# An encoder block in split fp32: two more plain up-projection pairs, and operand sums of 24 activation blocks made early and kept in DRAM

## The chip, the core and the metric

The kernel runs as one program on one core of a Trainium2 chip. The metric is device time in microseconds, the median of several executions. TensorE (PE) multiplies; VectorE (DVE), ScalarE (ACT) and GpSimd (POOL) prepare and finish; SyncE (SP) issues most loads, POOL issues the saves and the accumulating loads.

## The reference

One layer of a bidirectional encoder over 512 positions of width 2048. The part that matters here is its feed-forward half:

```
x = x + concat(RMSNorm_A(attn), RMSNorm_B(conv)) @ W_o
h = RMSNorm(x)                            # 512 x 2048
u = conv3_centred(h @ W_up) + b           # 512 x 11264: 5632 gates, 5632 values
y = silu(u[:, :5632]) * u[:, 5632:]       # 512 x 5632
x = x + y @ W_down                        # 512 x 2048
out = RMSNorm(x)                          # the last one
```

All of it is float32.

## The kernel before, in words

Everything is kept transposed, 128 channels on the partitions and the 512 positions along the row. A float32 product is made of three matmuls: each operand is split into a rounded part (`hi`, a copy on ACT) and the rest (`lo`, a subtraction on DVE), and `hi·hi + hi·lo + lo·hi` is accumulated. Each weight unit of 128x1024 (512 KB) is loaded by SP into one of eight `raw` buffers and split into one of three `hi`/`lo` pairs of buffers. The program is a list of `Item`s, one for each stretch of PE work on one weight unit. `run` walks the list and keeps loads and splits a few items ahead; an item's `posts` are other work, written into the program behind the item or some items later. A scheduler of the framework then sets the final order on each engine from this; within an engine the instructions run in that order.

The feed-forward half has 44 pairs `f` of 128 gate and 128 value columns. The first `NPLAIN` pairs are plain: four items of 24 matmuls of 512 columns each (line 242). The others go through `seven`, a scheme that makes a 2x2 block product with seven products in place of eight: seven items of 24 matmuls of 256 columns each (line 864), for which weights are added and subtracted (`raw<-raw` on DVE, accumulating `raw<-wall` loads on POOL, line 888) and the operand too is needed in sums and differences of its blocks. `make_operands` builds these: from two 128x512 tiles `a` and `b` it makes differences of 256 columns (lines 229, 836, 837) and splits them into seven tiles of fp32r. One call of it is called an operand set here.

Operand sets are made in two places. Before the first `seven` pair, `normed_operands` is called eight times from posts of the plain items: it loads two tiles of the residual back from DRAM (`t<-xr`), scales them (line 828), and makes the set; all eight sets are used by every `seven` pair. In the down-projection the 44 activation blocks are taken in chunks of eight: five chunks with four output groups `m` of seven items each (`down_seven`, again line 864), and the last four blocks plain. Each of the five chunks needs four operand sets. For that, `gated` saves each finished activation block to DRAM (`act<-t`, line 780, on POOL), and `sums_of` loads two of them back (`t<-act`, line 785, on SP) and calls `make_operands`: for the first chunk from posts of the last up-projection pair, for each later chunk from posts of the chunk ahead of it, one set in each `m`. `fetch_xr` loads the residual, to which the down-projection adds, in 32 pieces (line 989) at the end of the up-projection. All 128x512 tiles (2 KB a partition) share one pool of 80 buffers.

The two places where one part hands over to the next are called the first crossing here (plain to `seven` pairs) and the second crossing (up- to down-projection).

Of the kernel before, what the change touches and what calls it, by code (L numbers as in the profile page):

```python
# [62 lines left out]
SCALE = float(1.0 / np.sqrt(np.float32(NOPE + ROPE)))  # L63
UW = 1024
NT = 80
NPLAIN = 4
AHEAD = 4
HT = T // 2
FILL = 3
# [100 lines left out]
def encoder_block(ctx: ExitStack, tc: tile.TileContext, gx, wall, vecs, rot, out):  # L170
# [9 lines left out]
    def tile_r():  # L180
        return tp.tile([P, T], F32R, tag="t", name="t")

    def pair():
        return tile_r(), tile_r()

    def ztile():
        return tp.tile([P, T], F32, tag="t", name="t")
# [36 lines left out]
    def col(name, i):  # L224
        c = _VEC[name] + i
        return vec[:, c:c + 1]

    def tt(o, a, b, op, eng=None):
        (eng or nc.vector).tensor_tensor(out=o, in0=a, in1=b, op=op)  # L229

    def split(dst, src, eng=None):
        nc.scalar.copy(out=dst[0], in_=src)  # L232
        tt(dst[1], src, dst[0].bitcast(F32), ALU.subtract, eng)
# [87 lines left out]
    items = []  # L321
# [221 lines left out]
    v, qr, qk, pr = {}, {}, {}, {}  # L543
# [227 lines left out]
    def half(t, i):  # L771
        return t[:, i * HT:(i + 1) * HT]
# [3 lines left out]
    def save(name, src):  # L776

        saved[name] = [(dram.tile([P, T], F32, name=f"{name[0]}{name[1]}_{i}"), t.dtype) for i, t in enumerate(src)]
        for (o, _), t in zip(saved[name], src):
            nc.gpsimd.dma_start(o, t.bitcast(F32))  # L780

    def restore(name):
        ts = [tp.tile([P, T], dt, tag="t", name="t") for _, dt in saved[name]]
        for o, (d, _) in zip(ts, saved[name]):
            nc.sync.dma_start(o.bitcast(F32), d)  # L785
        return ts

    def conv_up(u, t, s, f):
# [4 lines left out]
        if s == 0:  # L793
            nc.scalar.activation(u, u, AF.Silu)

    def gated(us, f):
        tt(us[1], us[0], us[1], ALU.mult)
        if f < starts[last]:
            save(("act", f), [us[1]])
            return  # L800
        a = pair()
        split(a, us[1])
        save(("act", f), a)


    def up_plain(f, by_half):

        us, its = [None, None], []
        for s in range(2):
            def conv(ps, s=s):  # L810
                t = ztile()
                us[s] = ztile()
                if s == 0:
                    tt(t, ps, rx.r, ALU.mult)
                else:
                    nc.vector.scalar_tensor_tensor(out=t, in0=ps, scalar=-1.0, in1=rx.r, op0=ALU.mult, op1=ALU.mult)
                conv_up(us[s], t, s, f)

            lag = 5 if (f, s) == (0, 0) else 1
            its.append(proj16([("up", s, f, j) for j in range(2)], h2, [(lag, conv)] + [(lag + 1, lambda ps: gated(us, f))] * s, True))  # L820
        return its

    operands = []

    def normed_operands(i):
        (a,), (b,) = restore(("xr", 2 * i)), restore(("xr", 2 * i + 1))
        for k, t in ((2 * i, a), (2 * i + 1, b)):
            nc.vector.scalar_tensor_tensor(out=t, in0=t, scalar=col("ffn_g", k), in1=rx.r, op0=ALU.mult, op1=ALU.mult)  # L828
        operands.append(make_operands(a, b))

    def make_operands(a, b):

        u, v = ztile(), ztile()
        tt(half(u, 0), half(a, 0), half(a, 1), ALU.subtract)
        tt(half(u, 1), half(b, 1), half(a, 1), ALU.subtract)
        nc.vector.scalar_tensor_tensor(out=half(v, 0), in0=half(a, 0), scalar=-1.0, in1=half(u, 1), op0=ALU.mult, op1=ALU.subtract)  # L836
        nc.vector.scalar_tensor_tensor(out=half(v, 1), in0=half(v, 0), scalar=-1.0, in1=half(b, 0), op0=ALU.mult, op1=ALU.subtract)  # L837
        one = tile_r()
        split((half(one, 0), half(one, 1)), half(a, 0))
        got = {1: (half(one, 0), half(one, 1))}  # L840
        for src, names in ((u, (5, 7)), (v, (6, 4)), (b, (2, 3))):
            p = pair()
            split(p, src)
            for j, q in enumerate(names):
                got[q] = half(p[0], j), half(p[1], j)
        return got

    banks = []
# [87 lines left out]
    def up_seven(f):  # L936
        tg, tv, us = [], [], [None, None]

        def c11(ps):
            tg.append(ztile())  # L940
            nc.scalar.copy(out=half(tg[0], 0), in_=ps)

        def c22(ps, other):
            tv.append(ztile())
            tt(half(tv[0], 1), ps, other, ALU.add)

        def c21(ps, other):
            tt(half(tv[0], 0), ps, other, ALU.add)
            us[1] = ztile()
            conv_up(us[1], tv[0], 1, f)  # L950

        def c12(ps):
            nc.scalar.copy(out=half(tg[0], 1), in_=ps)
            us[0] = ztile()
            conv_up(us[0], tg[0], 0, f)

        units = {f"a{s + 1}{j + 1}": ("up", s, f, j) for s in range(2) for j in range(2)}
        its = seven(f, units, {"c11": c11, "c22": c22, "c21": c21, "c12": c12}, operands)
        its[-1].posts.append((2, lambda: gated(us, f)))
        return its  # L960

    starts = [sum(CHUNKS[:i]) for i in range(len(CHUNKS))]
    last = len(CHUNKS) - 1
    plain = []
    for f in range(0, NPLAIN - 2):
        plain += [it for its in up_plain(f, False) for it in its]
    four = [it for f in range(NPLAIN - 2, NPLAIN) for it in up_plain(f, True)]
    plain += [its[j] for j in range(2) for its in four]
    plain.insert(2, Item(rx.sums, posts=[(1, rx.chain)]))
    plain.insert(4, Item(rx.spread, posts=[(1, rx.take)]))  # L970
    for i in range(KD // 2):
        plain[(6, 7, 8, 9, 10, 14, 15, 16)[i]].posts.append((0, lambda i=i: normed_operands(i)))
    plain[-2].posts.append((0, mark))
    items.extend(plain)
    for f in range(NPLAIN, NF):
        items.extend(up_seven(f))


    acts, xt, sums = {}, {}, {}
# [4 lines left out]
    def fetch_xr(m):  # L984
        for a in range(2):
            for h in range(2):
                xt[m, a, h] = ztile()
                for e in range(2):
                    nc.sync.dma_start(half(xt[m, a, h], e), half(saved[("xr", 4 * m + 2 * e + a)][0][0], h))

    def sums_of(c, i):
        (a,), (b,) = (restore(("act", starts[c] + 2 * i + j)) for j in range(2))
        sums.setdefault(c, []).append(make_operands(a, b))

    def down_seven(c, m):
        def onto(a, h, op):
            def f(ps):
                tt(xt[m, a, h], xt[m, a, h], ps, op)
            return f

        units = {f"a{i + 1}{j + 1}": ("ds", c, m, i, j) for i in range(2) for j in range(2)}
        posts = {"s7": onto(1, 1, ALU.subtract), "u2": onto(1, 0, ALU.subtract), "c11": onto(0, 0, ALU.add),
                 "c22": onto(1, 1, ALU.subtract), "c21": onto(1, 0, ALU.subtract), "c12": onto(0, 1, ALU.add)}
        return seven(m, units, posts, sums.setdefault(c, []), T, True)

    at = len(items) - 7
    for i, j in enumerate((0, 2, 4, 5)):
        items[at + j].posts.append((0, lambda i=i: sums_of(0, i)))
    for m in range(KD // 4):
        items[at + (5, 6, 6, 6)[m]].posts.append((0, lambda m=m: fetch_xr(m)))  # L1010
    for c in range(last):
        for m in range(KD // 4):
            its = down_seven(c, m)
            if c + 1 < last:
                its[2].posts.append((0, lambda c=c, m=m: sums_of(c + 1, m)))
            items.extend(its)

    def fetch(f):
# [99 lines left out]
```

## Time and profile before

| | before |
|---|---|
| median of 3 runs | 2070.59 us (2070.19 to 2071.48) |
| profiled execution | 2071.46 us, its span 2069.7 us |
| mean granted TensorE clock | 0.991 |
| PE busy | 2023.5 us, 98% |
| DVE busy | 1557.1 us, 75% |
| ACT busy | 985.5 us, 48% |
| POOL busy | 212.6 us, 10% |
| HBM traffic | 140 GB/s over the span |

Shares of busy time are means over the whole program; a matmul that is slow or waits for its data can be counted as busy, so the count of matmuls in a stretch of 100 us says more on PE than its share.

### The profile page before, as it was taken

How to read it: one execution, taken by the hardware profiler on the slowest of the kernel's cores; microseconds unless marked ns; L12 is line 12 of the kernel's file. 1: busy time of each engine (PE TensorE's matmuls, PEld its weight loads, DVE VectorE, ACT ScalarE, POOL GpSimd, SP SyncE). 2: the span in 40 equal slices, each digit the busy share in tenths (PEclk: the TensorE clock that was granted, in tenths of full speed). 3: DMA queues.
4: the chain of work that ended last, by engine and by line, in shares of the span. 5: the costliest groups of instructions: out<-in, count | busy, mean ns of one | idle time of the engine just before them, and what ended most of it. 6: DMA issues, size and time to landing. Idle time of an engine off the chain costs nothing.

```text
span 2069.7 us, 34189 instructions
## 1 busy us (share of the span) xinstructions
PE 2023.5 (98%) x13970; PEld 1881.3 (91%) x13970; DVE 1557.1 (75%) x1905; ACT 985.5 (48%) x1374; POOL 212.6 (10%) x206
## 2 busy tenths in 40 slices
PE   8999999999999998999999999999998999999997
PEld 7888888888888887999999999999997999999997
DVE  7375776764557588878788787787887998988776
ACT  5253543432224345555555555555554554544454
POOL 5001323220001000000000000000000100000000
PEclk9999999999999998999999999999999999999999
DMA  7222222123444343554544545445456876767642
GB/s 260 95 87 76 79 70 89 65 92 97 140 141 139 130 160 96 153 154 132 163 134 147 160 132 158 141 140 169 130 157 193 235 197 172 207 161 212 173 123 82
DMA packets 94444, 291.85 MB, mean 141 GB/s; under 512 B 10704, under 2 KB 19024, under 8 KB 94288
## 3 DMA queue, kind: packets, MB, share of 16 engines
q1 hardware_dynamic: 77648, 230.95, 32.6%
q0 software_dynamic: 16640, 58.73, 14.6%
q8 instruction: 109, 1.79, 0.3%
q14 instruction: 47, 0.39, 0.1%
HBM read 268.66 MB, written 20.97 MB: 140 GB/s over the span
## 4 chain that ended last, share of the span: by engine, by line
PE 88%; DVE 6%; DMA 2%; issue 1%; ACT 0%; SPq 0%; DVEq 0%; ACTq 0%
PE ps L864 51%; PE ps L242 37%; DVE t L229 2%; DVE lo L229 2%; DMA t<-act 2%; DVE raw L229 1%; DMA t<-xr 0%; ACT hi L232 0%; DVE t L836 0%; DVE t L837 0%; DMA raw<-wall 0%; DVE t L828 0%; DVE t L486 0%; DVE t L487 0%; SPq L785 0%
## 5 line engine op out<-in xcount | busy, mean ns | idle before, releaser
L864 PE MATMUL ps<-t,hi 128*128 128x256 f32 x6720 | 1188.9, 281 | 26.2 <-DVE t L229 9.3
L864 PEld LDWEIGHTS ps<-t,hi 128*128 128x128 f32 x6720 | 1024.3, 189 | 30.8 <-DVE t L229 11.5
L864 PE MATMUL ps<-t,lo 128*128 128x256 f32 x3360 | 923.5, 280 | 1.7 <-DVE lo L229 1.7
L232 ACT CAST hi<-raw 128x1024 fp32r<-128x1024 f32 (+1 forms) x550 | 573.9, 1046 | 731.7 <-PE ps L864 264.1
L229 DVE TENSOR_TENSOR lo<-raw,hi 128x1024 fp32r<-128x1024 f32 (+1 forms) x549 | 676.1, 1233 | 214.4 <-ACT hi L232 204.3
L864 PEld LDWEIGHTS ps<-t,lo 128*128 128x128 f32 x3360 | 626.3, 189 | 2.4 <-DVE lo L229 2.3
L242 PE MATMUL ps<-t,hi 128*128 128x512 f32 x1968 | 613.8, 394 | 5.3 <-ACT t L237 4.5
L242 PEld LDWEIGHTS ps<-t,hi 128*128 128x128 f32 x1968 | 369.8, 188 | 87.6 <-ACT t L237 5.4
L242 PE MATMUL ps<-t,lo 128*128 128x512 f32 x992 | 385.9, 392 | 0.0
L229 DVE TENSOR_TENSOR t<-ps,t 128x512 f32<-128x512 f32 (+2 forms) x257 | 143.3, 571 | 161.7 <-PE ps L242 99.0
L229 DVE TENSOR_TENSOR t<-t 128x512 fp32r<-128x512 f32 (+4 forms) x356 | 222.6, 642 | 35.1 <-DMA t<-act 14.4
L242 PEld LDWEIGHTS ps<-t,lo 128*128 128x128 f32 x992 | 186.6, 188 | 41.9 <-issue 0.5
L229 DVE TENSOR_TENSOR raw<-raw 128x1024 f32<-128x1024 f32 x160 | 194.9, 1218 | 0.5
L242 PE MATMUL ps<-t 128*128 128x256 f32 (+1 forms) x642 | 108.7, 326 | 0.0
L232 ACT CAST t<-t 128x512 fp32r<-128x512 f32 (+2 forms) x149 | 81.9, 577 | 54.5 <-DVE t L229 28.5
L242 PEld LDWEIGHTS ps<-t 128*128 128x128 f32 x642 | 95.2, 190 | 10.3
L229 DVE TENSOR_TENSOR t<-t,ps 128x512 f32<-128x512 f32 x128 | 86.5, 681 | 18.1 <-PE ps L864 17.1
L780 POOL DMA_DIRECT2D act<-t x48 | 27.4, 571 | 698.9 <-DVE t L229 661.4
L229 POOL TENSOR_TENSOR t<-t 128x512 f32<-128x512 f32 x39 | 65.3, 1674 | 73.4 <-DVE t L229 40.1
L888 POOL DMA_DIRECT2D raw<-wall x60 | 52.2, 870 | 194.8 <-ACT t L920 71.3
L341 ACT ACTIVATE t<-l 128x512 f32<-128x512 f32 x44 | 27.5, 627 | 47.2 <-DVE l L229 47.0
L894 POOL DMA_DIRECT2D raw<-wall x20 | 17.3, 864 | 316.7 <-DVE lo L229 201.8
(81 smaller groups left out, 826.2 us busy)
## 6 DMA issues: line engine op xcount, KB each, us to landing
raw<-wall SPq DMA_DIRECT2D x372, 512.0 KB, 4.0
raw<-wall POOLq DMA_DIRECT2D x80, 512.0 KB, 5.9
act<-t POOLq DMA_DIRECT2D x48, 256.0 KB, 2.5
t<-act SPq DMA_DIRECT2D x48, 256.0 KB, 5.2
t<-gx SPq DMA_DIRECT2D x16, 256.0 KB, 3.8
xr<-l POOLq DMA_DIRECT2D x16, 256.0 KB, 2.4
t<-xr SPq DMA_DIRECT2D x16, 256.0 KB, 3.8
t<-xr SPq DMA_DIRECT2D x32, 128.0 KB, 3.8
```

Source lines behind the costliest of these rows:

```text
L229: (eng or nc.vector).tensor_tensor(out=o, in0=a, in1=b, op=op)
L232: nc.scalar.copy(out=dst[0], in_=src)
L242: nc.tensor.matmul(ps, lhsT=w, rhs=x, start=start, stop=stop)
L341: nc.scalar.activation(sq, src, AF.Square)
L780: nc.gpsimd.dma_start(o, t.bitcast(F32))
L864: nc.tensor.matmul(half(ps, e), lhsT=w[a][:, c:c + P], rhs=ops[k][q][b], start=start and e == k == i == 0, stop=k == n - 1 and i == 2, ski ...
L888: nc.gpsimd.dma_start(raw["a21"], wall[UIDX[units["a22"]]], accum_op=ALU.add)
L894: nc.gpsimd.dma_start(raw["s"], wall[UIDX[units["a12"]]], accum_op=ALU.add)
```

## The change

Two more pairs are plain (`NPLAIN` 6), and the eight calls of `normed_operands` are spread over the 26 items that the plain part now has. For the blocks of chunks 2, 3 and 4 (`f` from 16 to 39, named in `EARLY`), `gated` no longer saves the activation block: at each odd `f` it makes the operand set of the two blocks at once, in the up-projection, and saves its seven tiles (`sums`). `sums_of` then loads the seven finished tiles for these chunks; for chunks 0 and 1 it does what it did. The chunks are taken in the order 2, 0, 3, 1, 4. There are 28 operand sets in all as before; 12 of them move from the down-projection into the up-projection, so that 84 tiles of sums are saved in place of 24 blocks, and loaded in place of 24. `make_operands` now gives back its seven tiles, and `views` names their halves.

```diff
-NPLAIN = 4
+NPLAIN = 6
+ORDER = [2, 0, 3, 1, 4]
+EARLY = (2, 3, 4)
...
+    kept = {}
+
     def gated(us, f):
         tt(us[1], us[0], us[1], ALU.mult)
+        if f // 8 in EARLY:
+            kept[f] = us[1]
+            if f % 2:
+                save(("sums", f // 2), make_operands(kept.pop(f - 1), kept.pop(f)))
+            return
         if f < starts[last]:
             save(("act", f), [us[1]])
             return
...
-        operands.append(make_operands(a, b))
+        operands.append(views(make_operands(a, b)))
...
         split((half(one, 0), half(one, 1)), half(a, 0))
-        got = {1: (half(one, 0), half(one, 1))}
-        for src, names in ((u, (5, 7)), (v, (6, 4)), (b, (2, 3))):
+        ts = [one]
+        for src in (u, v, b):
             p = pair()
             split(p, src)
+            ts += p
+        return ts
...
-        plain[(6, 7, 8, 9, 10, 14, 15, 16)[i]].posts.append((0, lambda i=i: normed_operands(i)))
+        plain[(6, 7, 9, 11, 13, 18, 20, 22)[i]].posts.append((0, lambda i=i: normed_operands(i)))
...
     def sums_of(c, i):
-        (a,), (b,) = (restore(("act", starts[c] + 2 * i + j)) for j in range(2))
-        sums.setdefault(c, []).append(make_operands(a, b))
+        f = starts[c] + 2 * i
+        if c in EARLY:
+            ts = restore(("sums", f // 2))
+        else:
+            (a,), (b,) = (restore(("act", f + j)) for j in range(2))
+            ts = make_operands(a, b)
+        sums.setdefault(c, []).append(views(ts))
...
-        items[at + j].posts.append((0, lambda i=i: sums_of(0, i)))
+        items[at + j].posts.append((0, lambda i=i: sums_of(ORDER[0], i)))
...
-    for c in range(last):
+    for c, after in zip(ORDER, ORDER[1:] + [None]):
         for m in range(KD // 4):
             its = down_seven(c, m)
-            if c + 1 < last:
-                its[2].posts.append((0, lambda c=c, m=m: sums_of(c + 1, m)))
+            if after is not None:
+                its[2].posts.append((0, lambda c=after, m=m: sums_of(c, m)))
             items.extend(its)
```

The scheduler's order of the built program shows what this does at three places. The first is DVE at the first crossing. Here `t_5999` and `t_6001` are the residual tiles of the eighth (last) operand set, the rows up to `t_6023` build it, `lo_6105` is the first split of weights for a `seven` item, and L816, L486 and L487 belong to the convolution of the last plain pairs. Before:

```order
L828 SCALAR_TENSOR_TENSOR t_5999<-t_5999,vec_83,t_5394 128x512
L229 TENSOR_TENSOR t_5970<-t_5901,t_5970 128x512
L828 SCALAR_TENSOR_TENSOR t_6001<-t_6001,vec_83,t_5394 128x512
L229 TENSOR_TENSOR t_6005<-t_5999 128x256
L229 TENSOR_TENSOR t_6005<-t_6001,t_5999 128x256
L836 SCALAR_TENSOR_TENSOR t_6006<-t_5999,t_6005 128x256
L229 TENSOR_TENSOR t_6011<-t_5999,t_6011 128x256
L837 SCALAR_TENSOR_TENSOR t_6006<-t_6006,t_6001 128x256
L229 TENSOR_TENSOR t_6015<-t_6005,t_6014 128x512
L229 TENSOR_TENSOR t_6019<-t_6006,t_6018 128x512
L229 TENSOR_TENSOR lo_6105<-raw_5898,hi_6104 128x1024
L229 TENSOR_TENSOR t_6023<-t_6001,t_6022 128x512
```

After the change `t_6197` and `t_6199` are the residual tiles of the eighth set and `lo_6225` and `lo_6262` are splits of weights for the last plain items:

```order
L837 SCALAR_TENSOR_TENSOR t_6197<-t_6197,vec_83,t_5394 128x512
L231 TENSOR_TENSOR lo_6225<-raw_6078,hi_6224 128x1024
L837 SCALAR_TENSOR_TENSOR t_6199<-t_6199,vec_83,t_5394 128x512
L231 TENSOR_TENSOR t_6203<-t_6197 128x256
L231 TENSOR_TENSOR t_6203<-t_6199,t_6197 128x256
L845 SCALAR_TENSOR_TENSOR t_6204<-t_6197,t_6203 128x256
L231 TENSOR_TENSOR t_6209<-t_6197,t_6209 128x256
L846 SCALAR_TENSOR_TENSOR t_6204<-t_6204,t_6199 128x256
L231 TENSOR_TENSOR t_6213<-t_6203,t_6212 128x512
L231 TENSOR_TENSOR lo_6262<-raw_6136,hi_6261 128x1024
L231 TENSOR_TENSOR t_6217<-t_6204,t_6216 128x512
L231 TENSOR_TENSOR t_6221<-t_6199,t_6220 128x512
```

Before, the eighth set stands around the split of the first `seven` weights. After, it stands around the last splits for plain items; the four convolutions of the last plain pairs come behind it.

The second place is DVE in the up-projection at an odd `f` of `EARLY`. `t_9122` and `t_8890` are the two activation blocks, `lo_` are splits of weights; L231, L845 and L846 are lines 229, 836 and 837 of before. After:

```order
L231 TENSOR_TENSOR lo_9257<-raw_8960,hi_9256 128x1024
L231 TENSOR_TENSOR raw_9351<-raw_9190,raw_9192 128x1024
L231 TENSOR_TENSOR t_9195<-t_9122,t_8890 128x256
L231 TENSOR_TENSOR lo_9289<-raw_8993,hi_9288 128x1024
L845 SCALAR_TENSOR_TENSOR t_9196<-t_8890,t_9195 128x256
L231 TENSOR_TENSOR lo_9322<-raw_9084,hi_9321 128x1024
L231 TENSOR_TENSOR t_9201<-t_8890,t_9201 128x256
L846 SCALAR_TENSOR_TENSOR t_9196<-t_9196,t_9122 128x256
L231 TENSOR_TENSOR t_9205<-t_9195,t_9204 128x512
L231 TENSOR_TENSOR t_9209<-t_9196,t_9208 128x512
L231 TENSOR_TENSOR t_9213<-t_9122,t_9212 128x512
L231 TENSOR_TENSOR t_9358<-ps_6302,t_9262 128x256
```

The pieces of one operand set (`t_9195` to `t_9213`) stand between the splits of weights; before, the same stretch held only the splits and the sums of the weights.

On POOL, saves and accumulating loads of weights alternated, one of each for each pair; after the change, in the pairs of `EARLY`, two loads of weights in a row (line 904 of the changed kernel) are followed by the seven saves of one set (line 782).

The third place is SP at the second crossing, where L259 are loads of weights. Before:

```order
L259 DMA raw_15314<-wall 128x1024
L259 DMA raw_15371<-wall 128x1024
L785 DMA t_15242<-act0_0_5498 128x512
L785 DMA t_15244<-act1_0_5744 128x512
L259 DMA raw_15635<-wall 128x1024
L259 DMA raw_15637<-wall 128x1024
L785 DMA t_15342<-act2_0_6035 128x512
L785 DMA t_15344<-act3_0_6113 128x512
L259 DMA raw_15678<-wall 128x1024
L785 DMA t_15430<-act4_0_6347 128x512
L785 DMA t_15432<-act5_0_6581 128x512
L259 DMA raw_15734<-wall 128x1024
```

After, from the same place on (L261 are the weights; L787 is the load of `sums`):

```order
L787 DMA t_15593<-sums10_5_10219 128x512
L787 DMA t_15594<-sums10_6_10220 128x512
L261 DMA raw_15771<-wall 128x1024
L261 DMA raw_15773<-wall 128x1024
L261 DMA raw_15814<-wall 128x1024
L787 DMA t_15635<-sums11_0_10713 128x512
L787 DMA t_15636<-sums11_1_10714 128x512
L787 DMA t_15637<-sums11_2_10715 128x512
L787 DMA t_15638<-sums11_3_10716 128x512
L787 DMA t_15639<-sums11_4_10717 128x512
L787 DMA t_15640<-sums11_5_10718 128x512
L787 DMA t_15641<-sums11_6_10719 128x512
```

Before, the eight loads of `act` alternate with weights. After, the seven tiles each of `sums8`, `sums9` and `sums10` stand in one piece behind the first four weights of the down-projection, then come three weights, the seven tiles of `sums11`, and directly behind them the 32 residual loads.

## Rows read from the trace of the kernel before

**Rows 1.** Windows by stage: bounds; us, PE, PEld, DVE, ACT, POOL busy (x count); PEclk; DMA; GB/s.

```profile
600.00:700.00 100.00, 100.00 (x439) 82.12 (x438) 64.39 (x84) 38.99 (x50) 8.99 (x16) 1.00 0.42 137
700.00:800.00 100.00, 90.89 (x413) 74.50 (x412) 77.68 (x126) 42.72 (x62) 2.56 (x4) 0.95 0.38 124
800.00:900.00 100.00, 100.00 (x835) 100.00 (x834) 82.00 (x92) 55.77 (x78) 7.21 (x10) 0.98 0.50 145
900.00:1000.00 100.00, 100.00 (x852) 100.00 (x851) 80.13 (x87) 55.61 (x76) 7.15 (x10) 1.00 0.50 146
1500.00:1600.00 100.00, 90.26 (x730) 89.15 (x729) 78.46 (x97) 54.67 (x80) 7.39 (x11) 0.95 0.57 171
1600.00:1700.00 100.00, 94.70 (x795) 93.40 (x794) 95.28 (x136) 52.66 (x71) 9.79 (x12) 1.00 0.78 217
1700.00:1800.00 100.00, 98.06 (x829) 97.29 (x828) 91.52 (x127) 51.01 (x66) 7.74 (x9) 1.00 0.69 184
1800.00:1900.00 100.00, 98.25 (x831) 97.80 (x829) 84.17 (x103) 45.04 (x52) 9.43 (x11) 1.00 0.72 197
1900.00:2000.00 100.00, 100.00 (x851) 100.00 (x850) 79.44 (x88) 46.40 (x55) 7.24 (x9) 1.00 0.64 173
```

**Rows 2.** Windows again, of the matmuls of line 242, then of line 864.

```profile
700.00:800.00 100.00, 81.59 (x359) 66.47 (x357) 0.95 0.38 124
...
700.00:800.00 100.00, 9.47 (x54) 8.03 (x55) 0.95 0.38 124
```

**Rows 3.** The chain of waits at the first crossing: start, length, what.

```profile
792.95 0.66 DVE t L828
...
796.34 0.34 DVE t L837
...
798.60 1.44 PE ps L864 x5
```

**Rows 4.** The chain of waits at the second crossing.

```profile
1581.14 7.73 DMA t<-act
...
1592.10 4.63 PE ps L864 x21
1596.73 2.78 DMA t<-xr
```

**Rows 5.** Windows around the two crossings.

```profile
784.00:800.00 16.00, 6.89 (x33) 5.27 (x32) 14.03 (x25) 6.89 (x11) 0.54 (x1) 0.70 0.05 17
1570.00:1610.00 40.00, 29.50 (x209) 27.98 (x208) 31.93 (x51) 20.91 (x34) 2.86 (x4) 0.87 0.63 194
```

**Rows 6.** DVE's waits between 1560 and 1900 us: total, times, longest.

```profile
DVE t L229 <- DMA t<-act: 14.4, 15, 4.8
```

**Rows 7.** DVE's groups by form, 700 to 800 us: count, busy, mean ns.

```profile
L229 DVE TENSOR_TENSOR t<-t 128x512 fp32r<-128x512 f32 x24 | 15.9, 685 | 1.5 <-ACT t L232 1.4
...
L229 DVE TENSOR_TENSOR t<-t 128x256 f32<-128x256 f32 x16 | 6.1, 417 | 0.0
...
L836 DVE SCALAR_TENSOR_TENSOR t<-t 128x256 f32<-128x256 f32 x8 | 3.4, 422 | 0.2
```

**Rows 8.** POOL's groups by form, 900 to 1500 us.

```profile
L888 POOL DMA_DIRECT2D raw<-wall x31 | 27.1, 875 | 63.4 <-ACT t L920 61.3 <-ACT hi L232 2.0
L780 POOL DMA_DIRECT2D act<-t x31 | 17.3, 559 | 505.6 <-DVE t L229 505.6
```

**Rows 9.** SP's timeline at the second crossing: start, us spent on issuing, what.

```profile
1564.64 0.85 SPq L785 DMA_DIRECT2D t<-act  x2
...
1580.66 0.96 SPq L785 DMA_DIRECT2D t<-act  x2
...
1593.76 1.93 SPq L785 DMA_DIRECT2D t<-act  x2
1595.73 19.61 SPq L989 DMA_DIRECT2D t<-xr  x32
```

**Rows 10.** The page's DMA issues: count, KB each, us to landing.

```profile
t<-act SPq DMA_DIRECT2D x48, 256.0 KB, 5.2
```

More of the change, by code (lines that the diff above doesn't have):

```diff
@@ L839, in make_operands, with views @@
         split((half(one, 0), half(one, 1)), half(a, 0))
-        got = {1: (half(one, 0), half(one, 1))}
-        for src, names in ((u, (5, 7)), (v, (6, 4)), (b, (2, 3))):
+        ts = [one]
+        for src in (u, v, b):
             p = pair()
             split(p, src)
+            ts += p
+        return ts
+    def views(ts):
+        got = {1: (half(ts[0], 0), half(ts[0], 1))}
+        for i, names in enumerate(((5, 7), (6, 4), (2, 3))):
             for j, q in enumerate(names):
-                got[q] = half(p[0], j), half(p[1], j)
+                got[q] = half(ts[1 + 2 * i], j), half(ts[2 + 2 * i], j)
         return got
```

## The prediction

> **What bounds the kernel now.** I read the windows by stage first and counted matmuls, since their busy time is modelled and their count is not. Undisturbed, PE starts 852 matmuls of 256 columns in 100 us, one in .1174 us (the row from 900), and 439 of 512 columns, one in .2278 us (the row from 600) [rows 1]. So a `seven` pair (168 matmuls) costs 19.72 us and a plain pair (96) 21.87 us. In such stretches no other engine decides: DVE is busy 64% and 80%.
>
> The time lost lies where the counts fall short. **First crossing:** between 700 and 800 us PE did 359 wide and 54 narrow matmuls [rows 2], worth 81.8 + 6.3 us, so 11.9 us are gone; from 800 to 900 another 17 of 852 are missing, 2.0 us: 13.9 in all. **Second crossing:** between 1570 and 1610 there are 209 matmuls [rows 5] where 40 / .1174 = 341 fit: 132 missing, 15.5 us. **Chunks:** from 1500 to 1900 the rows have 730, 795, 829 and 831, so 223 missing, 26.2 us; without the crossing's 15.5 that leaves 10.7 us, spread over the first four chunks. From 1900, in the chunk that makes no operand sets, nothing is missing [rows 1]. These counts include what the lower clock after a stall costs: the granted clock was .70 of 2.4 GHz while PE starved at the first crossing and .87 around the second [rows 5].
>
> What PE waits for is read from the chains. At the first crossing it is DVE: scaling the residual (L828), differences (L837) of the last operand set and then a split of weights stand right before PE's next matmul at 798.60 [rows 3], and DVE was busy 14.0 of 16 us [rows 5]. At the second it is a DMA: DVE stands behind `t<-act` for 7.73 us, weights' splits stand behind that on DVE, and PE resumes at 1592.10 [rows 4]. Of DVE's waits from 1560 to 1900 us, 14.4 us in 15 times are for `t<-act` [rows 6].
>
> **The change, part by part.**
>
> *Two more plain pairs.* Each costs 21.87 − 19.72 = 2.15 us more PE work: **+4.3**. No cover, since PE is the bound there.
>
> *First crossing.* An operand set is three splits of 512 columns at .685 us and five operations of 256 columns at .417 to .422 [rows 7]: 3 × .685 + 5 × .418 = 4.15 us of DVE, with two scalings 5.6. The eight sets are the same, but are spread over 26 items. In the order before, the last set stands around the first `seven` split, so that all of it is on PE's path; after, it stands around `lo_6225` and `lo_6262`, the last two splits of plain weights. At least two plain items of 24 × .2278 = 5.5 us are then still ahead of PE, 11 us, against some 6 us for the rest of the set and 7 to 8 us for the four convolution passes and the first split behind it. Much fits, and little is left over. Bounds: 0 (as before) and 13.9 (all). I take 13.4: **−13.4**. If the cover were gone, the stall would come back at up to its old size.
>
> *Up-projection.* Twelve sets of 4.15 us, 49.8 us of DVE, move under two `seven` pairs each. DVE idles 19.87 in 100 us there [rows 1], so 7.8 us in two pairs (39.4 us); after the set 3.7 us are left and DVE is at 90.5%. ACT, at 56%, has room. The inputs are already in SBUF, so no load is waited for. The pieces stand between splits of weights in the order, so a split is pushed back by a few operations of .4 to .7 us, not by the whole set. The nearest row for the danger is the down-projection's own: 16 sets cost 10.7 us, .67 each; by that, 12 would cost 8.0. But DVE stood at 95% there and waited for loads [rows 1, 6], which the new place does not. Between 0 and 8.0 I take **+1.5**.
>
> *Saves.* 84 tiles on POOL in place of 24. A save takes POOL .56 us and an accumulating load .88 [rows 8]; seven saves are 3.9 us in 39.4, and in POOL's order they stand behind both loads of weights, about a pair's length before the next load. 0. The Trainium skill ("SBUF — State Buffer", section "A bandwidth-pool intuition that's wrong") speaks against this part: a DMA issued from GpSimd needs the port that DVE can hold, and its 620 ns became about 3100 ns beside a DVE copy. By it seven saves would last an estimated 21.7 us. The trace does not agree so far: the saves took .56 us beside a DVE that was 80% busy.
>
> *Second crossing.* DVE makes no set there any more, so nothing of its queue stands behind a load: the 7.73 us and what follows from them go. What can be late instead is a tile that PE itself needs. The loads of `sums8` take the place of the first `t<-act`, which SP issued at 1564.64 [rows 9], some 3 us before the last pair starts on PE (PE resumes at 1592.10 with the sixth of its products; five took 5 × 2.82 us and some 10 us of the stall, so it began at about 1568). Call that start T. 21 tiles at .48 us an issue (two in .96 [rows 9]) are 10.1 us, until T + 7. Then three loads of weights wait for their buffers, which splits free at one a product, 2.82 us; I put `sums11` at T + 14.5. Its seven issues take 3.4 us, and a tile lands 5.2 us after its issue [rows 10]: T + 23.1. PE needs it one microsecond into the first product of the down-projection, at T + 19.7 + 1.05 = T + 20.8. Late by 2.3. The 32 residual loads come behind at .61 us each [rows 9]; the first eight land at about T + 28, when the fourth product's result (T + 31) asks for them. I take 2 us of stall in place of 15.5: **−13.5**. Bounds: 0 and, with every tile issued as slowly as the slowest two (.97 each, 1.93 for two [rows 9]), 28 × .49 = 13.7 us more, so a crossing as bad as before.
>
> *Chunks.* Eight sets stay in the down-projection (for chunks 0 and 1, made while chunks 2 and 3 run) of the 16 that lay in the chunks. At .67 each: **−5.4**. Bounds: −10.7, and 0 if what remains is as crowded.
>
> Sum: 4.3 − 13.4 + 1.5 − 13.5 − 5.4 = −26.5. The profiled execution took 2071.46 us, 1.8 more than its span and .9 more than the median; so 2071.46 − 26.5 = 2045.0, or **2044** beside the median.
>
> **The rivals.**
>
> *Loads bunch at the second crossing.* 28 tiles (7.3 MB), seven weights and 32 pieces leave SP one after the other. For it: the DMA share was already .63 with 8 tiles there [rows 5], and one pair of issues took 1.93 us. Against it: three of four sets are issued 15 us ahead. At the upper bound the crossing costs 11 to 14 us more than I took: 2044 + 11 = 2055. Chance .17.
>
> *The first crossing's stall moves rather than goes.* The four convolution passes and the last set are the same DVE work, and the eighth set can only start when a tile or its residual is free; if it starts two items late, half to all of 13.9 remains: 2044 + 7 to 13, 2051 to 2057. Chance .10.
>
> *DVE becomes the bound of the up-projection* (the other side). A split for PE stands behind pieces of the set, twelve times. It is not faster any more from (26.5 − 4.1) / 12 = 1.9 us more a set than I took, and if all 4.15 lay bare, 12 × 4.15 − 1.5 = 48 us come on top: 2092. For it: the row at 95% DVE lost 6.7 us in 100 [rows 1]. Against it: 7.8 us of idle time for 4.15 of work. Chance .09, two thirds of it with a loss.
>
> *POOL is held up.* If each save took five times its .56 us, seven would take some 20 us; they start when the set is ready, some 8 us behind the last load of weights, and the next load would come 8 to 10 us late, twelve times: about 100 us slower, 2145. That is the page's rule; the saves' .56 us speaks against it. Chance .02.
>
> **How the numbers follow.** The forecast has .62, with its own range 2038 to 2051 (the up-projection's 0 to 8, the chunks' bounds). If every stall went, it would be 4.3 − 13.9 − 15.5 − 10.7 = −35.8, 2035. The first two rivals reach to 2057, both in part to 2060. Range 2035 to 2060, with some .12 above it. A measurement of this kernel tells about .2%, 4.1 us, from no change. Faster: .62 + .17 + .10 + .02 of the third = .91; same .03; slower .06.
>
> **What would show it.** First crossing: no window with under 80% of its matmuls before the `seven` pairs. Up-projection: 852 in each 100 us with DVE at 90%; under 835 the third rival is right. Second crossing: no DVE wait for a load; PE waiting for a DMA of `sums` for 0 to 3 us. Chunks: losses only in the second and third place, half of before. I am wrong if a PE wait for splits shows in each pair of `EARLY`, or if SP's issues stretch past the start of the down-projection.

## The result, and the profile after

The changed kernel took 2135.86 us (median, 2134.8 to 2136.25) against 2070.39 us of the kernel before: 65.5 us slower. The two medians make 1.0316; the ratio estimated from all runs is 1.0344 (95% interval 1.0268 to 1.042). The prediction was 2044 us, range 2035 to 2060.

The windows by stage of the changed kernel, in the columns of [rows 1], show where.

```profile
700.00:800.00 100.00, 100.00 (x441) 81.86 (x440) 75.32 (x119) 42.31 (x60) 3.11 (x5) 1.00 0.41 138
800.00:900.00 100.00, 100.00 (x770) 95.34 (x769) 79.88 (x95) 52.21 (x72) 6.34 (x9) 1.00 0.48 139
900.00:1000.00 100.00, 100.00 (x885) 100.00 (x884) 83.06 (x91) 58.35 (x81) 7.19 (x10) 1.00 0.53 156
1000.00:1100.00 100.00, 95.56 (x812) 95.16 (x811) 78.76 (x89) 54.39 (x76) 9.38 (x14) 0.97 0.52 154
1100.00:1200.00 100.00, 91.11 (x734) 90.31 (x733) 76.83 (x94) 52.40 (x75) 11.28 (x18) 0.95 0.48 144
1200.00:1300.00 100.00, 90.32 (x716) 89.30 (x714) 75.24 (x91) 49.91 (x71) 12.11 (x19) 0.93 0.49 148
1300.00:1400.00 100.00, 87.51 (x700) 86.71 (x701) 73.58 (x90) 50.41 (x76) 15.17 (x25) 0.93 0.56 164
1400.00:1500.00 100.00, 91.13 (x732) 90.12 (x731) 74.74 (x91) 51.49 (x73) 11.27 (x18) 0.95 0.51 160
1500.00:1600.00 100.00, 91.12 (x727) 90.31 (x726) 76.02 (x93) 51.76 (x74) 11.29 (x18) 0.93 0.48 143
1600.00:1700.00 100.00, 91.72 (x746) 90.73 (x745) 72.27 (x83) 47.58 (x64) 10.71 (x15) 0.97 0.88 274
1700.00:1800.00 100.00, 90.30 (x745) 89.30 (x744) 79.88 (x102) 42.96 (x54) 7.71 (x9) 0.97 0.79 235
1800.00:1900.00 100.00, 99.68 (x845) 99.44 (x844) 82.96 (x100) 45.06 (x52) 8.61 (x10) 1.00 0.73 198
```

Three things are to be seen. First, the stall of the first crossing is gone: 441 wide matmuls from 700 to 800 us, and the 770 from 800 to 900 are what the last wide ones, until about 826 us, and the narrow ones behind them make without a gap. Second, from 900 to 1000 there are 885 narrow matmuls, where the kernel before had 852 in its undisturbed stretches [rows 1]: a faster pace, at the same granted clock of 1.00. Third, from 1000 to 1600, in the pairs of `EARLY`, the counts sum to 4421 where 852 each would be 5112: 691 missing, 81 us by the .1174 us of [rows 1]. From 1600 to 1900, around and behind the second crossing, 2336 are there of 2556: 220 missing, 26 us, no less than the 26.2 us of before.

As a sum: two plain pairs +4.3, first crossing −13.9, the 33 extra matmuls of 900 to 1000 −3.9, up-projection +81.1, second crossing and chunks 25.8 − 26.2 = −.4: +67 us, for 65.5 measured (the extra matmuls before 900 us are not in it).

What PE waited for in the up-projection, from PE's waits between 1000 and 1600 us (total, times, longest):

```profile
PE ps L880 <- ACT t L936: 53.2, 12, 4.4
```

One wait, the same twelve times. L936 is the copy in `keep`, by which ACT empties a PSUM bank (a bank in which PE's products are summed; the copies are `s7` and `u2`) before PE may go on in it. ACT's timeline in one of the twelve, pair 24 (start, length, what, idle before and its releaser):

```profile
1202.47 1.05 ACT L234 CAST hi<-raw 128x1024 fp32r<-128x1024 f32 x1 [2.06 <-PE ps L880]
1205.06 1.04 ACT L234 CAST hi<-raw 128x1024 fp32r<-128x1024 f32 x1 [1.54 <-DVE lo L231]
1206.01 0.92 ACT L234 CAST t<-t 128x256 fp32r<-128x256 f32 x2
1208.07 1.14 ACT L234 CAST t<-t 128x512 fp32r<-128x512 f32 x2 [1.14 <-DVE t L846]
1209.11 0.64 ACT L936 COPY t<-ps 128x256 f32<-128x256 f32 x2
```

PE's wait of 4.4 us ended with the first of the two copies at about 1209.5, so PE had been done with all ahead of it, the products to be copied among them, since 1205.1; ACT began the copies (x2) only at 1209.11. Ahead of them on ACT stand a split of weights, which waited 1.54 us for DVE, and the operand set's four copies, the last two of which waited 1.14 us for L846 on DVE. Of the 4.0 us from 1205.1 to 1209.11 the split took 1.0, the set's copies 2.0 and the wait for DVE 1.1. PE stood still for 4.4 us, and ran at a lower clock behind it: a short window of the same place,

```profile
1208.00:1216.00 8.00, 6.47 (x35) 6.47 (x36) 1.93 (x4) 1.96 (x5) 3.29 (x6) 0.58 1.00 337
```

with 35 matmuls in 8 us (68 fit) at a mean granted clock of .58 of 2.4 GHz, that is mostly at 1.2 GHz. So each of the twelve costs 81.1 / 12 = 6.8 us, counted by 852.

At the second crossing the waits are others than before [rows 4]. PE's waits there, in three stretches (1640 to 1660, 1685 to 1700, 1755 to 1785 us):

```profile
PE ps L880 <- DMA t<-sums: 2.4, 1, 2.4
```

```profile
PE ps L880 <- ACT ps L931: 3.2, 1, 3.2
```

```profile
PE ps L880 <- ACT hi L234: 8.2, 2, 8.0
```

The first, 2.4 us for the last tiles of `sums`, is the one that the prediction priced at 2.3. The last, 8.2 us, stands in the second chunk (chunk 0). SP's timeline (start, time on issuing, what), SP's waits from 1749 to 1763 us and ACT's from 1640 to 1800 us explain it:

```profile
1629.19 14.46 SPq L787 DMA_DIRECT2D t<-sums  x21
...
1646.55 8.58 SPq L787 DMA_DIRECT2D t<-sums  x7
...
1744.13 4.39 SPq L787 DMA_DIRECT2D t<-sums  x4
1748.87 0.33 SPq L261 DMA_DIRECT2D raw<-wall  x1
1749.55 12.50 SPq L787 DMA_DIRECT2D t<-sums  x10
1762.40 1.03 SPq L787 DMA_DIRECT2D t<-act  x2
```

```profile
SPq L787 <- DMA t<-sums: 4.9, 9, 1.9
SPq L787 <- DMA raw<-wall: 4.4, 2, 3.4
```

```profile
ACT t L234 <- DMA t<-act: 15.4, 3, 12.8
```

The activation blocks of chunk 1's first operand set were issued at 1762.40, behind the tiles of chunk 3's sums. SP took 12.5 us for the last ten of these: between 1749 and 1763 us it waited 9.3 us in all for earlier loads to land. ACT stood behind these blocks for up to 12.8 us, with the weights' splits for PE behind it.

The saves on POOL cost what was said: the page's rows

```profile
L782 POOL DMA_DIRECT2D sums<-t x84 | 46.4, 552 | 38.9 <-ACT t L234 25.3
```

give .55 us each, beside the .56 of [rows 8].

### The profile page after: what moved, and what is told of

Same layout as the page of the kernel before. It is cut to its first block, busy times and chain, and to the rows that moved or that the text cites. A ratio compares the mean times of both kernels' runs of the same rounds, so it can differ in the third digit from the quotient of the medians.

```text
span 2134.5 us, 34139 instructions
## 1 busy us (share of the span) xinstructions
PE 2045.0 (96%) x13826; PEld 1892.0 (89%) x13826; DVE 1544.5 (72%) x1893; ACT 976.7 (46%) x1358; POOL 242.9 (11%) x264
## 5 line engine op out<-in xcount | busy, mean ns | idle before, releaser
L880 PE MATMUL ps<-t,hi 128*128 128x256 f32 x6496 | 1164.2, 284 | 71.5 <-ACT t L936 53.2
L234 ACT CAST hi<-raw 128x1024 fp32r<-128x1024 f32 (+1 forms) x544 | 566.6, 1046 | 809.5 <-PE ps L880 254.8
L880 PE MATMUL ps<-t,lo 128*128 128x256 f32 x3248 | 900.6, 282 | 0.0
L231 DVE TENSOR_TENSOR lo<-raw,hi 128x1024 fp32r<-128x1024 f32 (+1 forms) x543 | 668.3, 1234 | 197.6 <-ACT hi L234 187.9
L244 PE MATMUL ps<-t,hi 128*128 128x512 f32 x2096 | 653.9, 394 | 4.9 <-ACT t L239 4.7
L244 PE MATMUL ps<-t,lo 128*128 128x512 f32 x1056 | 411.0, 392 | 0.0
L231 DVE TENSOR_TENSOR t<-ps,t 128x512 f32<-128x512 f32 (+3 forms) x255 | 143.1, 575 | 233.2 <-PE ps L880 117.0
L231 DVE TENSOR_TENSOR t<-t 128x512 f32<-128x512 f32 (+4 forms) x356 | 221.5, 640 | 31.0 <-ACT t L343 10.7
L231 DVE TENSOR_TENSOR raw<-raw 128x1024 f32<-128x1024 f32 x154 | 187.9, 1220 | 0.8
L231 DVE TENSOR_TENSOR t<-t,ps 128x512 f32<-128x512 f32 x128 | 87.0, 684 | 40.8 <-PE ps L880 36.1
L231 POOL TENSOR_TENSOR t<-t 128x512 f32<-128x512 f32 x39 | 63.8, 1636 | 76.1 <-DVE t L231 40.1
L782 POOL DMA_DIRECT2D act<-t x24 | 14.3, 595 | 341.0 <-DVE t L231 283.2
L782 POOL DMA_DIRECT2D sums<-t x84 | 46.4, 552 | 38.9 <-ACT t L234 25.3
```

The costliest lines, as they stand in the source:

```text
L244: nc.tensor.matmul(ps, lhsT=w, rhs=x, start=start, stop=stop)
L880: nc.tensor.matmul(half(ps, e), lhsT=w[a][:, c:c + P], rhs=ops[k][q][b], start=start and e == k == i == 0, stop=k == n - 1 and i == 2, ski ...
```

## The experiments

Theory A: ACT's order. The set's copies stand ahead of the copies that PE waits for. Theory B: DVE has too much to do. Theory C: the saves, on POOL or as traffic. Later come theory P, that the pace follows from whether PE was interrupted, and rival Q, that it follows from the number of plain pairs or from where the tiles lie. The kernel before took 2069 to 2072 us beside each of these runs.

**Six plain pairs alone.**

```diff
-ORDER = [2, 0, 3, 1, 4]
-EARLY = (2, 3, 4)
+ORDER = [0, 1, 2, 3, 4]
+EARLY = ()
```

> Six plain pairs and the new places of the eight normed operand sets, but all 44 activation blocks saved as before, chunks in natural order, 20 sets made in the down-projection. This isolates the first crossing. All theories of the loss in the up-projection expect 852 matmuls in each 100 us there. If the first crossing's 13.9 us are gone for 4.3 us of plain work, the time is 2070.4 + 4.3 - 13.9 = 2061 (2058 to 2064); if the stall only moved, 2068 to 2075.

2034.53 us (2033.8 to 2036.45), ratio .9825 (.981 to .9839): 27 us better than expected. Its windows:

```profile
1000.00:1100.00 100.00, 100.00 (x885) 100.00 (x884) 83.44 (x91) 58.00 (x80) 7.19 (x11) 1.00 0.50 146
...
1500.00:1600.00 100.00, 88.08 (x732) 86.49 (x732) 84.80 (x113) 53.93 (x78) 10.56 (x15) 0.95 0.72 212
```

The 885 of above hold through the whole up-projection, from 826 to 1540 us; then the second crossing stalls, and the counts fall much as they did before. At 852 the same matmuls would take 714 us × (885 / 852 − 1) = 27.7 us more, about the 26.5 us that were missing from my sum.

**The operand sets written later.**

```diff
-            if f % 2:
-                save(("sums", f // 2), make_operands(kept.pop(f - 1), kept.pop(f)))
...
         its[-1].posts.append((2, lambda: gated(us, f)))
+        if f // 8 in EARLY and f % 2:
+            its[-1].posts.append((6, lambda: save(("sums", f // 2), make_operands(kept.pop(f - 1), kept.pop(f)))))
```

> The changed kernel, with the operand sets of the up-projection written four items later (posts six items behind the pair's last item in place of two), so that on ACT both copies that empty a PSUM bank for PE (the keep copies) stand ahead of the set's splits. Same work, same saves. Theory A (ACT's queue order): the twelve waits of 4.4 us of PE for the keep copy go, with the clock lost behind them, 691 missing matmuls or 81 us in all: 2055 (2045 to 2065). Theory B (DVE has too much to do there): the wait moves to a split of weights and most stays: 2100 to 2136. Theory C (the saves on POOL or their DMA traffic hold something up): 2125 to 2136.

2040.36 us (2039.6 to 2041.25), ratio .9851 (.9834 to .9867). ACT's order at pair 18, in the changed kernel and in this one (`COPY t<-ps` of L936 and L934 are the `keep` copies, `CAST t` the set's):

```
L234 CAST hi_9321<-raw_9084 128x1024
L234 CAST t_9201<-t_8890 128x256
...
L234 CAST t_9212<-t_9122 128x512
L936 COPY t_9262<-ps_9231 128x256
L936 COPY t_9294<-ps_6302 128x256
```

```
L934 COPY t_9227<-ps_9196 128x256
L234 CAST hi_9253<-raw_8993 128x1024
L934 COPY t_9259<-ps_6302 128x256
L234 CAST hi_9286<-raw_9084 128x1024
L955 COPY t_9290<-ps_9161 128x256
L234 CAST t_9329<-t_8890 128x256
```

The windows of this kernel:

```profile
1100.00:1200.00 100.00, 100.00 (x885) 100.00 (x884) 92.16 (x113) 62.57 (x90) 16.87 (x27) 1.00 0.61 193
...
1500.00:1800.00 300.00, 279.02 (x2294) 276.53 (x2293) 233.41 (x283) 133.17 (x166) 26.11 (x33) 0.97 0.78 234
...
1660.00:1680.00 20.00, 11.57 (x79) 11.07 (x78) 10.00 (x15) 4.91 (x7) 0.00 (x0) 0.75 0.84 281
```

From 1000 to 1500 us PE waits for nothing, and does 885 in each 100 us with DVE 92% busy. So B is wrong: the same work, written four items later, costs nothing there, and A holds. The set stands later on DVE too, so this run by itself does not part ACT's order from DVE's; the timeline of the twelve waits does, in which 1.1 of 4.0 us are for DVE and the rest is ACT's own work ahead of the copies. The waits also broke the faster pace, so the 81 us counted by 852 are too few: the two runs are 2135.9 − 2040.4 = 95.5 us apart. The time is below A's range because A's sum went by 852, and without the waits the pace stays at 885. It is 6 us slower than the run before nevertheless: from 1500 to 1800 there are 2294 matmuls of 2556, 31 us lost, with a wait of 8.4 us behind `t<-act` as in the changed kernel (the row from 1660).

**One keep copy ahead.** As the run before, with 4 in place of 6.

> As the run before, but the sets are written only two items later, so that on ACT the first keep copy stands ahead of the set's splits and the second behind them. Theory A: a smaller wait for the second copy, 1 to 3 us in each of twelve pairs with its clock, 2065 to 2110, between the other two. Theory B and C: no different from the changed kernel, 2125 to 2136.

2095.9 us (one run), between the two. PE's waits from 1000 to 1600 us:

```profile
PE ps L878 <- ACT hi L234: 20.2, 12, 1.8
PE ps L878 <- ACT t L934: 5.3, 13, 1.8
```

The wait shrank to at most 1.8 us, in the range given, but most of it was for a split of weights (its copy on ACT) and not for the `keep` copy: both stand behind copies of the set on ACT. Theories B and C expected no difference from the changed kernel.

**Saves without sets.** This kernel saves the two activation blocks in place of the sums, and leaves the making of the twelve sets out.

```diff
-                save(("sums", f // 2), make_operands(kept.pop(f - 1), kept.pop(f)))
+                x, y = kept.pop(f - 1), kept.pop(f)
+                save(("sums", f // 2), [x, y, x, y, x, y, x])
+                saved[("sums", f // 2)] = [(d, F32R) for d, _ in saved[("sums", f // 2)]]
```

> The changed kernel without the making of the twelve sets in the up-projection: the two activation blocks themselves are saved seven times in all in place of the seven tiles, and the down-projection multiplies these. The values are not the reference's. 84 saves on POOL and all the traffic stay, DVE's and ACT's work of the sets is gone. Theory A and B: no waits in the up-projection, 2055 (2045 to 2065). Theory C: the waits stay, 2125 to 2136.

2035.63 us (one run), 885 in each window and no wait of PE from 1000 to 1500 us with all 84 saves there, .55 us each. C is wrong; the time is below the range of A and B for the reason given at the run with late sets.

**The stall of the first crossing brought back**, on the run with six plain pairs alone.

```diff
-        plain[(6, 7, 9, 11, 13, 18, 20, 22)[i]].posts.append((0, lambda i=i: normed_operands(i)))
+        plain[(14, 15, 16, 17, 18, 22, 23, 24)[i]].posts.append((0, lambda i=i: normed_operands(i)))
```

> As the run with six plain pairs alone (2034.5 us), but the eight normed operand sets are posted as late as in the kernel before (items 14 to 18 and 22 to 24 of 26), to bring the stall at the first crossing back. Theory P (the pace of PE follows from whether it was interrupted: 885 narrow matmuls in 100 us while nothing has stalled it, 852 after a stall): the stall's 13.9 us and 714 us at 852 in place of 885, 27 us: 2075 (2068 to 2080), with 852 in the windows of the up-projection. Rival Q (the pace follows from the number of plain pairs or where the tiles lie): 885 stay, 2048 (2044 to 2052).

2072.05 us (one run):

```profile
800.00:900.00 100.00, 90.89 (x646) 85.11 (x645) 85.15 (x114) 51.14 (x75) 5.45 (x8) 0.95 0.43 134
900.00:1000.00 100.00, 100.00 (x852) 100.00 (x851) 80.11 (x87) 55.33 (x76) 7.17 (x10) 1.00 0.48 146
```

With the same six plain pairs and the stall, the pace is 852 again through the whole up-projection, as P expected. Of Q this excludes the number of pairs; late posts may also lay tiles elsewhere, and for that the next runs have the better sign, a change of pace within one run.

**Five plain pairs.** `NPLAIN = 5`, with the sets at items 6, 7, 9, 11, 13, 15, 17 and 18.

> As the run with six plain pairs alone (2034.5 us), with five, and the eight sets at items 6 to 18 of 22. One plain pair costs 21.8 us and one of seven products at 885 in 100 us 19.0. Theory P: if nothing stalls at the first crossing, 885 and 2034.5 - 2.8 = 2031.7 (2030 to 2034); if something does, 852 and some 2060 to 2073. Rival Q: 852 because five plain pairs place the tiles anew, about 2059.

2059.96 us (2059.04 to 2063.37), ratio .9945 (.9931 to .996): at the edge of P's second case. PE waited once at the crossing, between 810 and 830 us, and the pace changed there, from 108 matmuls in 12 us ahead of the wait to 104 behind it:

```profile
PE ps L880 <- DVE lo L231: 0.7, 1, 0.7
```

```profile
804.00:816.00 12.00, 12.00 (x108) 12.00 (x107) 12.00 (x16) 8.95 (x14) 0.01 (x1) 1.00 0.06 20
819.00:831.00 12.00, 12.00 (x104) 12.00 (x103) 11.63 (x15) 7.18 (x10) 0.54 (x1) 1.00 0.60 204
...
900.00:1000.00 100.00, 100.00 (x851) 100.00 (x851) 79.57 (x87) 55.80 (x77) 7.15 (x10) 1.00 0.49 147
```

Q gave the same time for this run; what speaks against it is that the pace fell in the middle of the run, at the wait.

**Chunk order 2, 0, 1, 3, 4**, on top of the late sets.

> As the run with late sets (2040.4 us), with the chunks in the order 2, 0, 1, 3, 4, so that the loads of activation blocks for chunk 1's sets no longer stand on SP behind the 28 loads of chunk 3's sums. Theory A (DVE and ACT stand behind these loads, and the splits of weights behind them: 8.4 us of PE's wait and the lower clock after it, 91 of 170 matmuls missing in 20 us): 10.7 us less, 2030 (2028 to 2033). Rival (the same 12 sets and loads only collide elsewhere): 2037 to 2042.

2025.67 us, ratio .9785 (.9762 to .9808): faster than the kernel before and the changed one, and below theory A's range. The wait behind `t<-act` is gone from PE's waits. Its four runs fall in two groups, 2021.4 and 2021.8, 2029.5 and 2030.7; the second lies in the range. The profiled run is of the first:

```profile
1500.00:1700.00 200.00, 186.53 (x1540) 184.25 (x1539) 167.39 (x215) 98.45 (x131) 19.23 (x25) 0.98 0.81 239
1700.00:1800.00 100.00, 100.00 (x885) 100.00 (x884) 77.04 (x80) 41.20 (x42) 8.61 (x10) 1.00 0.87 259
```

From 1700 to 1900 it runs at 885, which no other profile of this study does there for so long. 200 us of that at 852 would take 7.7 us more, about the distance of the groups; that the slower runs are at 852 there no trace shows.

**The residual loads spread.**

```diff
-    for m in range(KD // 4):
-        items[at + (5, 6, 6, 6)[m]].posts.append((0, lambda m=m: fetch_xr(m)))
+    items[at + 5].posts.append((0, lambda: fetch_xr(0)))
...
+            if c == ORDER[0] and m < KD // 4 - 1:
+                its[0].posts.append((0, lambda m=m: fetch_xr(m + 1)))
```

> As the run before, and of the 32 residual loads only the eight of the first output group stay at the second crossing; the others are written into the first chunk, one group ahead each. Takes 24 issues of .6 us and 3.1 MB out of the crossing. Theory R (loads bunch at the crossing: waits for sums, residual and accumulating weights of some 8 us and the clock behind them): 4 to 10 us less than the run before, 2020 to 2026. Rival (the stalls there come from the weights' and sums' loads alone): within 2 us of the run before.

2027.11 us (2026.65 to 2028.99), ratio .9785 (.9771 to .98). From 1500 to 1700 it did 1558 matmuls for 1540 of the run before, 2 us; behind that it ran at 852, so the two times differ by the pace as well. PE's wait for `t<-sums` stayed at 2.8 us in both. So the residual loads carry at most a small part of the crossing's loss; theory R's 4 to 10 us are not there.

**Short interruptions of PE**, on the kernel with six plain pairs alone and on the kernel before.

```diff
...
-                product(bank_of(name, start), w, q, start, ops)
+                ps = bank_of(name, start)
+                if pre is not None and q == 1:
+                    pre(ps)
+                product(ps, w, q, start, ops)
...
+                    pre=(lambda ps: mm(ps, ones, half(gates[f - 1][0], 1), True, True)) if f % 4 == 2 and 10 <= f < 40 else None)
...
```

> The run with six plain pairs alone (2034.5 us, 885 narrow matmuls in 100 us through the up-projection), with a short interruption of PE at eight places: ahead of the first product of pairs 10, 14, ... 38, PE multiplies ones by the gate half that ACT copies out of the pair before, so that it must wait for that copy, about a microsecond. Theory P (an interruption sets the pace): the windows go from 885 to 852 behind the first or second interruption, and some 20 us are lost for 8 to 16 us of waits: 2055 to 2070. Rival Q (the pace follows from where tiles lie): 885 everywhere between the interruptions, 2042 to 2050.

> The kernel before (2071 us, 852 throughout the up-projection, which begins with a stall) with the same eight interruptions of PE. Theory P with a pace that any interruption sets anew: some of the stretches behind an interruption run at 885, so that a part of 27 us comes back and the time is 2055 to 2085. If an interruption can only slow PE down, 852 everywhere and 2080 to 2087. Rival Q: the same 852 everywhere.

2065.25 us and 2081.04 us (one run each). In the first, PE waited eight times, .5 us at most:

```profile
PE ps L244 <- ACT t L975: 3.7, 8, 0.5
```

```profile
850.00:900.00 50.00, 50.00 (x443) 50.00 (x443) 40.13 (x44) 28.03 (x39) 4.34 (x6) 1.00 0.56 157
900.00:950.00 50.00, 49.54 (x419) 49.29 (x419) 40.93 (x45) 28.12 (x40) 2.87 (x4) 1.00 0.44 134
...
1000.00:1050.00 50.00, 50.00 (x427) 50.00 (x427) 41.27 (x46) 29.18 (x40) 2.87 (x4) 1.00 0.43 130
```

The first interruption, at 900 us, ends the pace of 443 in 50 us (885 in 100); from there on it is 419 with an interruption and 427 without, to the end of the up-projection. 640 us at 852 in place of 885 are 24 us, and eight interruptions the rest of the 31 us. That is P's case and outside Q's. In the kernel before, none of the eight brought 885 back, and the time is that of interruptions which can only slow PE down.

## Why the prediction was wrong

**First crossing (−13.4): right.** The eighth set no longer stands before PE's first narrow matmul, PE waits for nothing from 780 to 1000 us, and the 13.9 us are gone. What I did not know is that the stall had a second price: the pace of PE behind it. In the kernel before, the whole up-projection ran at the slower pace, and I took that, [rows 1]'s 852, for PE's limit. In the run with six plain pairs alone this was worth another 27.7 us.

**Up-projection (+1.5): the step that failed.** "ACT, at 56%, has room", and "a split is pushed back by a few operations". I weighed DVE's order and ACT's share, and read no row of ACT's order. A share says nothing on what stands behind a waiting instruction: the set's copies wait for DVE, and behind them stand the two copies that free PSUM for PE. It measured 81 us in place of 1.5. The third rival named the place and the number of times, but the wrong engine: DVE at 92% loses nothing when ACT's order is right (the run with late sets). Its sign, counts under 835, came, and would have put the loss down to DVE; only PE's waits told that it was ACT. The Trainium skill ("TensorE: Matmul & The Clock Gate", section "Architectural detail: the array is 16× 32×32, not 1× 128×128") says that ACT's queue is a strict FIFO. The trace agrees: two copies whose products were done by 1205.1 ran at 1209.11, behind a copy that had waited 1.14 us for DVE.

The trace of the kernel before had shown this wait already, at the second crossing, where operand sets were made beside the last up-projection pair. PE's waits from 1570 to 1610 us, and ACT's timeline there (L920 is the `keep` copy of that kernel):

```profile
PE ps L864 <- ACT hi L232: 6.1, 2, 5.9
PE ps L864 <- ACT t L920: 2.9, 1, 2.9
```

```profile
1579.59 1.65 ACT L232 CAST t<-t 128x512 fp32r<-128x512 f32 x3
1581.15 0.36 ACT L920 COPY t<-ps 128x256 f32<-128x256 f32 x1
1587.99 0.41 ACT L232 CAST t<-t 128x256 fp32r<-128x256 f32 x1 [6.48 <-DMA t<-act]
```

Three copies of a set stand right ahead of the copy that PE waited 2.9 us for, and PE's longest wait, 5.9 us, was for a split on ACT behind the set's copies. The prediction read this crossing as DVE's: its 7.73 us are the step of the chain, while DVE itself waited 4.8 us at most [rows 6], and ACT 6.5.

**Saves (0): right.** 84 saves of .55 us, and no loss with them alone. The five times longer DMA that the Trainium skill ("SBUF — State Buffer", section "A bandwidth-pool intuition that's wrong") gives beside a DVE copy is not seen here beside DVE's sums and differences, nor in the run with late sets, with DVE 92% busy: .55 us a save there too.

**Second crossing (−13.5) and chunks (−5.4): wrong, nothing was gained.** The single number for the tiles came out, 2.4 us for 2.3, but by luck: SP took 14.5 us for the 21 tiles and 8.6 for the seven, where I had 10.1 and 3.4, and the three weights between them held it up for 2.9 us where I had some 7.5. And I worked out one wait and took the rest for gone. 25.8 us stayed in place of 7.3: `t<-act` for chunk 1 moved behind 28 loads of sums on SP, where I had looked at the crossing only, as the first rival did too, and the longest wait also cost clock (.83 granted from 1760 to 1780 us). With the chunk order 2, 0, 1, 3, 4 that one is gone, and the loss from 1500 to 1700 is 164 matmuls, 19 us. What the remaining 19 us would need was not settled: spreading the residual loads gave 2 us of it.

**The total.** Had the sets been written later, the change would have given 2040.4 us, near the forecast, but partly by accident: a gain of pace that I did not foresee, against a gain at the second crossing that did not come.

## What to carry to other kernels

For work that is moved under another stage, read the order of every engine that it touches, and look for what stands behind its first wait; here four copies of about .5 us on a half-idle engine, twelve times, cost 81 us, and the same copies four items later cost nothing. Moving loads past others on one queue can hurt a chunk later, so follow each queue to the end of the stage. Treat a best pace seen in a trace as what this run reached, not as the engine's limit, when the stretch began with a stall.

## What the runs showed of the hardware

A stream of 128x256 matmuls, each with its own load of weights, ran at one of two paces at a granted clock of 1.00: 885 or 852 in 100 us, .113 or .1174 us each. It kept 885 for 714 us while nothing interrupted PE, and went to 852 after one wait of at most .5 us (pair 10 of the interrupted kernel) or .7 us (five plain pairs), for the rest of the stage. Fifteen further interruptions in two kernels, at the slower pace, never brought 885 back. Yet it did come back elsewhere: in the run with chunk order 2, 0, 1, 3, 4 from 1700 to 1900 us, and for 20 us (179 matmuls, where 172 are the slower pace) at 1580 in the run with six plain pairs alone and at 1360 in the changed kernel, each time behind a stretch in which PE had waited. What sets the pace inside PE, and what brings it back, stays open. So a short wait at the start of a long stage can cost 3.9% of the stage: the kernel with five plain pairs came out 28 us above the 2031.7 expected without a stall, after a wait of .7 us.
